# A hybrid trunk layer on one core: the first pass over the tokens in groups of four blocks

## The chip, the core and the metric

The kernel runs on one core of one Trainium2 chip. A core has five engines that run side by side, each with its own list of instructions in fixed order: TensorE (PE in the profile) multiplies matrices and transposes, VectorE (DVE), ScalarE (ACT) and GpSimd (POOL) work elementwise, and SyncE (SP) issues the transfers between memory and the core's on-chip memory (SBUF). PE writes its results to a small accumulation memory (PSUM) in banks of 128 x 512 floats; DVE and ACT read them from there. An engine that waits holds up everything behind it in its own list. The metric is the time of one execution on the device, in microseconds (us); lower is better.

## The reference, cut to what matters

One layer of a trunk over 2048 latent tokens and 256 context tokens of width 1024. Both are normalised, scaled and shifted, and one projection of the result `h` feeds two mixers, a gated delta net and a windowed attention; their outputs are gated, merged, projected and added to `x`.

```
h  = _rmsnorm(x, norm_w) * (1.0 + scale[:, None]) + shift[:, None]
hc = _rmsnorm(ctx, norm_w) * (1.0 + scale_c) + shift_c
...
qkv, beta_r, decay_r, kb, vb = _split_cols(h @ w_state, STATE_SIZES)
za, qb, zb, ga, gb = _split_cols(h @ w_rest, REST_SIZES)
...
kb = _axial_rope(_rmsnorm(kb.reshape(b, l, ATT_KV_HEADS, ATT_HD), k_norm_w), pos_row, pos_col)
```

The first pass, which the change touches, computes `h` for all tokens and from it the columns for beta, decay, and the attention's keys `kb` and values `vb`.

## The kernel before, in words

The tokens are 18 blocks of 128, two of the context and 16 of x. All products are made in split precision: each factor is a high part and a low part (the rounding's remainder), and three products (high x high, low x high, high x low) are summed in PSUM. `h` is kept on chip with the features on the partitions, as `hh` (high) and `hl` (low), one tile pair of [128, 8, 512] for each group of four blocks and one for the context.

At the start the modulation's `shift` and `scale` are computed from two halves of `w_mod` (16 loads of 512 KB, tile `wm`); the context's blocks are loaded and normalised meanwhile. Then the first pass runs, over pairs of blocks:

- `load_x` loads a block into an `xt` tile. There are four of these, shared by context and x.
- `norm_x` sums the block's squares, half a block on ACT (L295) and half on DVE (L298, both write only a throw-away tile `junk` and the sum `ss`), adds the two (POOL, L299), forms mean plus eps (POOL, L301) and the power -0.5 (POOL, L72, `rstd`), and scales the block in place (DVE, L303).
- `make_h` takes a pair: for each of the eight feature tiles PE transposes the two blocks into one PSUM bank (`hps`, four banks, L344), ACT evicts 128 x 256 with scale and shift into half of an `h32` tile (`h` in the profile, L345, two buffers), POOL rounds two feature tiles at once to `hh` (L347) and DVE takes the remainder `hl` (L348).
- `tm_dense` multiplies one block with 272 columns of `w_in`: 24 products (`tmps`, L374 to L376) into one of three accumulator banks.
- `state_pair` takes two blocks' accumulators: ACT copies beta and decay (`bg`, L431) and the values (`vst`, L433, remainder on DVE L434) and squares the keys (`sq`, L435); DVE sums, POOL forms the norm (`ssn`, L439 and L72), DVE multiplies (`xn`, L443, the last reader of the accumulators), DVE and POOL rotate (`t`, `cw`, L452 to L462), ACT and DVE split into `kh` (L464 to L466), PE transposes (`kt`, L472), ACT copies to `ks` (L473), and SP stores to `Vsp` and `Ksp`.

Behind the last block the weights of the next stage come in, and PE starts the long products for the convolutions, `lps` (L532 to L534).

The order of instructions on each engine is set when the program is built, by a scheduler that goes by its own estimates; tiles come from pools with fixed numbers of buffers, and a tile's next use waits for the last reader of its buffer.

## Time and profile before

| | |
|---|---|
| three runs | 2110.58, 2101.88, 2107.05 us; median 2107.05 |
| profiled execution, span from first to last instruction | 2106.8 us |
| mean granted PE clock | 0.981 |
| busy: PE, DVE, POOL, ACT | 1991.7, 1424.9, 773.2, 746.8 us |
| first pass: first and last product of a `tmps` kind | from 44.75 us to just ahead of 136.96 us |

The profiled execution has no time of its own beside its span; the span stands at the median of the runs. In the rows of the profile, a group is named by line, engine, operation and tile (`out<-in`), with its count; an arrow in a row of waits or at the end of a group names what the engine waited for last. Busy times of PE are modelled, since products overlap.

### The profile page before, as it was taken

To read this page: it belongs to the slowest core of one execution; us is meant where nothing else is said; L and a number is where in the kernel's file an instruction comes from. 1 tells how busy PE (TensorE), PEld (TensorE's weight loads), DVE (VectorE), ACT (ScalarE), POOL (GpSimd) and SP (SyncE) were. 2 spreads that over 40 slices of the span, in tenths; PEclk is the share of its full clock that TensorE was granted. 3 is DMA by queue.
4 is the path that set the end of the run, shared out by engine and by line. 5 is a ranking of instruction groups with operands and counts; after the bars stand their busy time and mean duration, and the time that the engine had idled before them with its cause. 6 is when DMAs were issued, how large, how long until landed. Compare 5 with 4: busy or idle time off the path is not lost.

```text
span 2106.8 us, 32857 instructions
## 1 busy us (share of the span) xinstructions
PE 1991.7 (95%) x11351; PEld 1647.6 (78%) x11351; DVE 1424.9 (68%) x2715; ACT 746.8 (35%) x1911; POOL 773.2 (37%) x919
## 2 busy tenths in 40 slices
PE   6999999999998799889979999999989999999999
PEld 3888888888986567667867888888868787878887
DVE  6888767767662799789846985634587777753322
ACT  6655555644440001001211223323575555441100
POOL 2852202355541355313322223322356343442321
PEclk8999999999999899999989999999999999999999
DMA  6552247755444533437667778763365545455542
GB/s 248 163 145 86 78 134 207 209 170 157 142 139 111 125 105 110 108 98 215 182 177 202 207 217 231 202 205 116 116 190 180 173 149 174 121 178 190 172 145 93
DMA packets 392591, 335.47 MB, mean 159 GB/s; under 512 B 83144, under 2 KB 318600, under 8 KB 392072
## 3 DMA queue, kind: packets, MB, share of 16 engines
q1 hardware_dynamic: 365000, 290.88, 48.1%
q10 hardware_dynamic: 27424, 42.48, 5.7%
q8 instruction: 90, 1.47, 0.3%
q14 instruction: 77, 0.63, 0.1%
HBM read 220.21 MB, written 111.49 MB: 157 GB/s over the span
## 4 chain that ended last, share of the span: by engine, by line
PE 66%; DMA 10%; DVE 9%; POOL 4%; SPq 4%; issue 4%; ACT 2%; POOLq 0%; DVEq 0%; ACTq 0%
PE rps L534 5%; PE rps L532 5%; PE rps L533 4%; PE lps L532 4%; PE lps L534 4%; PE lps L533 4%; PE ops L1272 3%; PE ops L1274 3%; PE ops L1273 3%; DMA wr<-in_w_in_dram 2%; PE pps L1187 2%; PE pps L1188 2%; PE pps L1189 2%; PE pt L922 2%; DVE N L735 2%
## 5 line engine op out<-in xcount | busy, mean ns | idle before, releaser
L532 PE MATMUL rps<-hh,wh 128*128 128x512 f32 x768 | 313.7, 409 | 6.2 <-DVE rt L798 4.9
L534 PE MATMUL rps<-hh,wl 128*128 128x512 f32 x768 | 311.3, 406 | 0.0
L533 PE MATMUL rps<-hl,wh 128*128 128x512 f32 x768 | 309.9, 403 | 0.0
L251 POOL TENSOR_SCALAR wh<-wr 128x512 fp32r<-128x512 f32 x120 | 103.7, 874 | 276.6 <-DMA wr<-in_w_in_dram 119.7
L796 ACT ACTIVATE rt<-rps 128x512 f32<-128x512 f32 x96 | 57.4, 598 | 386.9 <-PE rps L534 327.8
L532 PEld LDWEIGHTS rps<-hh,wh 128*128 128x128 f32 x768 | 147.3, 192 | 39.3 <-DVE rt L798 5.3
L534 PEld LDWEIGHTS rps<-hh,wl 128*128 128x128 f32 x768 | 147.2, 192 | 36.5 <-issue 2.0
L533 PEld LDWEIGHTS rps<-hl,wh 128*128 128x128 f32 x768 | 147.2, 192 | 32.7 <-issue 1.3
L532 PE MATMUL lps<-hh,wh 128*128 128x512 f32 (+1 forms) x448 | 171.9, 384 | 0.3 <-ACT y L632 0.3
L534 PE MATMUL lps<-hh,wl 128*128 128x512 f32 (+1 forms) x448 | 171.4, 383 | 0.0
L533 PE MATMUL lps<-hl,wh 128*128 128x512 f32 (+1 forms) x448 | 171.2, 382 | 0.0
L571 DVE SCALAR_TENSOR_TENSOR cacc<-y,cw,cacc 128x512 f32<-128x512 f32 (+1 forms) x224 | 161.5, 744 | 13.9 <-ACT cacc L569 10.8
L908 POOL TENSOR_SCALAR pr<-pr,sm 128x640 f32<-128x640 f32 (+1 forms) x128 | 99.2, 795 | 176.7 <-DVE sm L906 154.3
L252 DVE TENSOR_TENSOR wl<-wr,wh 128x512 fp32r<-128x512 f32 x120 | 96.6, 814 | 71.2 <-POOL wh L251 69.0
L926 DVE TENSOR_TENSOR pl<-pt,ph 128x512 fp32r<-128x512 f32 x156 | 106.7, 685 | 39.7 <-ACT ph L924 38.9
L924 ACT CAST ph<-pt 128x512 fp32r<-128x512 f32 x156 | 90.9, 585 | 113.0 <-PE pt L922 72.1
L898 DVE TENSOR_REDUCE sm<-sc 128x1 f32<-128x640 f32 (+1 forms) x128 | 101.7, 800 | 38.8 <-PE sc L896 38.2
L735 DVE TENSOR_TENSOR N<-N,btmp 128x62 f32<-128x62 f32 (+30 forms) x124 | 120.9, 975 | 2.8
L733 DVE TENSOR_TENSOR btmp<-N 128x62 f32<-128x62 f32 (+30 forms) x124 | 119.4, 963 | 3.0
L900 ACT ACTIVATE pr<-sc,sm 128x640 f32<-128x640 f32 (+1 forms) x128 | 100.2, 784 | 49.0 <-DVE sm L899 39.4
L1187 PE MATMUL pps<-yh,wph 128*128 128x512 f32 x256 | 104.0, 410 | 7.3 <-ACT yh L1169 5.3
L1188 PE MATMUL pps<-yl,wph 128*128 128x512 f32 x256 | 102.9, 402 | 0.2 <-DVE yl L1170 0.2
(312 smaller groups left out, 5061.0 us busy)
## 6 DMA issues: line engine op xcount, KB each, us to landing
wr<-in_w_in_dram SPq DMA_DIRECT2D x120, 256.0 KB
kw<-Ksp SPq DMA_DIRECT2D x28, 384.0 KB
x<-vsp SPq DMA_DIRECT2D x36, 256.0 KB
k<-ksp SPq DMA_DIRECT2D x34, 256.0 KB
kT<-kTsp SPq DMA_DIRECT2D x34, 256.0 KB
wm<-in_w_mod_dram SPq DMA_DIRECT2D x16, 512.0 KB
xt<-in_x_dram SPq DMA_DIRECT2D x16, 512.0 KB
dtl<-Dsp SPq DMA_DIRECT2D x32, 256.0 KB
```

Of the source, the lines that this page charges most:

```text
L251: G.tensor_scalar(wh[:, k:k + 4], wr, 1.0, 1.0, op0=ALU.mult, op1=ALU.mult)
L532: T.matmul(ps, lhsT=wh[:, k], rhs=xh[:, k], start=k == 0, stop=False)
L533: T.matmul(ps, lhsT=wh[:, k], rhs=xl[:, k], start=False, stop=False)
L534: T.matmul(ps, lhsT=wl[:, k], rhs=xh[:, k], start=False, stop=k == kt - 1)
L571: V.scalar_tensor_tensor(a, y[:, t:t + n], cw[:, m, t:t + 1], a, op0=ALU.mult, op1=ALU.add)
L733: V.tensor_tensor(tv, A[:, m + 1:, m].unsqueeze(2).to_broadcast([h1 + n, r, m]), A[:, m, 0:m].unsqueeze(1).to_broadcast([h1 + n, r, m]), o ...
L735: V.tensor_tensor(A[:, m + 1:, 0:m], A[:, m + 1:, 0:m], tv, op=ALU.add)
L898: V.tensor_reduce(sm[:, h, 0:1], s_, axis=AX.X, op=ALU.max)
L900: S.activation(p[:, h, :W + 256], s_, AF.Exp, scale=0.125, bias=sm[:, h, 1:2], accum_out=sm[:, h, 2:3])
L926: V.tensor_tensor(pl, pt, f32(ph), op=ALU.subtract)
L1187: T.matmul(ps, lhsT=wh[:, k, ms], rhs=hs[k], start=k == 0, stop=False)
L1188: T.matmul(ps, lhsT=wh[:, k, ms], rhs=ls[k], start=False, stop=False)
```

## The change

The first pass goes over groups of four blocks, four times, and not over pairs, eight times. `load_x` can be given the place to load to. `norm_x` takes all blocks of a group: ACT alone sums the squares of each block in one 128 x 1024 operation, the two small POOL operations and the power run once for the group, and then DVE scales the four blocks. `make_h` transposes four blocks into a bank, evicts 128 x 512 at once, and takes one feature tile in an `h32` tile (for the context still two, of 256). Group 0 and group 3 are loaded into the four `xt` tiles; groups 1 and 2 are loaded into the memory that later holds `hh` and `hl` of group 3, which is free until then. `tm_dense` and `state_pair` are as they were, two pairs to a group.

```diff
-        def load_x(c):
-            xt = px.tile([128, D], F32, name="xt")
+        def load_x(c, xt=None):
+            if xt is None:
+                xt = px.tile([128, D], F32, name="xt")
...
-        def norm_x(c, xt):
-            ss = px.tile([128, 2], F32, name="ss")
-            for j in range(2):
-                junk = px.tile([128, 512], BF16, name="junk", bufs=1)
-                xs = xt[:, j * 512:(j + 1) * 512]
-                if j == 0:
-                    S.activation(junk, xs, AF.Square, accum_out=ss[:, j:j + 1])
-                else:
-                    junk2 = px.tile([128, 512], BF16, name="junk2", bufs=1)
-                    V.scalar_tensor_tensor(junk2, xs, 1.0, xs, op0=ALU.mult, op1=ALU.mult, accum_out=ss[:, j:j + 1])
-            G.tensor_tensor(ss[:, 0:1], ss[:, 0:1], ss[:, 1:2], op=ALU.add)
-            ss = ss[:, 0:1]
-            G.tensor_scalar(ss, ss, 1.0 / D, EPS, op0=ALU.mult, op1=ALU.add)
-            rsq(rstd[:, c:c + 1], ss)
-            V.tensor_scalar(xt, xt, rstd[:, c:c + 1], None, op0=ALU.mult)
+        def norm_x(c, xts):
+
+            n = len(xts)
+            ss = px.tile([128, 4], F32, name="ss", bufs=2)
+            for j, xt in enumerate(xts):
+                junk = px.tile([128, D], BF16, name="junk", bufs=1)
+                S.activation(junk, xt, AF.Square, accum_out=ss[:, j:j + 1])
+            G.tensor_scalar(ss[:, :n], ss[:, :n], 1.0 / D, EPS, op0=ALU.mult, op1=ALU.add)
+            rsq(rstd[:, c:c + n], ss[:, :n])
+            for j, xt in enumerate(xts):
+                V.tensor_scalar(xt, xt, rstd[:, c + j:c + j + 1], None, op0=ALU.mult)
...
-            for k in range(0, KT, 2):
-                h32 = px.tile([128, 2, 256], F32, name="h32", bufs=2)
-                for i in range(2):
+            per = 512 // n
+            for k in range(0, KT, per):
+                h32 = px.tile([128, per, n], F32, name="h32", bufs=2)
+                for i in range(per):
...
-                    S.activation(h32[:, i, :n], ps[:, :n], AF.Identity, scale=modA[:, k + i, cc:cc + 1],
+                    S.activation(h32[:, i], ps[:, :n], AF.Identity, scale=modA[:, k + i, cc:cc + 1],
                                  bias=modB[:, k + i, cc:cc + 1])
-                G.tensor_scalar(hi[:, k:k + 2], h32[:, :, :n], 1.0, 1.0, op0=ALU.mult, op1=ALU.mult)
-                V.tensor_tensor(lo[:, k:k + 2], h32[:, :, :n], f32(hi[:, k:k + 2]), op=ALU.subtract)
+                G.tensor_scalar(hi[:, k:k + per], h32, 1.0, 1.0, op0=ALU.mult, op1=ALU.mult)
+                V.tensor_tensor(lo[:, k:k + per], h32, f32(hi[:, k:k + per]), op=ALU.subtract)
...
-        for gi in range(8):
-            xts = []
-            for j in range(2):
-                c = NCB + gi * 2 + j
-                with tc.issue_after(wm_dma.ins):
-                    xts.append(load_x(c))
-                norm_x(c, xts[j])
-            o = gi % 2 * 256
-            make_h(xts, hh[gi // 2][:, :, o:o + 256], hl[gi // 2][:, :, o:o + 256], 0)
-            if gi == 7:
+        for gi in range(4):
+            c = NCB + gi * 4
+            homes = [None] * 4
+            if gi in (1, 2):
+                four = hB2.tile([128, 4, D], F32, name="xt4", tag="hh3" if gi == 1 else "hl3")
+                homes = [four[:, j] for j in range(4)]
+            if gi == 3:
+                hh[3] = hB2.tile([128, KT, 512], F32R, name="hh3", tag="hh3")
+                hl[3] = hB2.tile([128, KT, 512], F32R, name="hl3", tag="hl3")
+            with tc.issue_after(wm_dma.ins):
+                xts = [load_x(c + j, homes[j]) for j in range(4)]
+            norm_x(c, xts)
+            make_h(xts, hh[gi], hl[gi], 0)
+            if gi == 3:
...
-            c = NCB + gi * 2
-            state_pair(c, [tm_dense(c + j, wh, wl, NST) for j in range(2)])
+            for i in (0, 2):
+                state_pair(c + i, [tm_dense(c + i + j, wh, wl, NST) for j in range(2)])
```

The scheduler's order changes with it, up to the last product of the pass; behind that, every engine's list is what it was, apart from line numbers. Three places follow.

ACT, around the context's finished products (`bg`, `vst`, `sq` of the context's two blocks read its finished products). Before:

```order
L345 ACTIVATE h_650<-hps,modB,modA 128x256
L295 ACTIVATE junk,ss<-xt 128x512
L345 ACTIVATE h_661<-hps,modB,modA 128x256 x2
L345 ACTIVATE h_672<-hps,modB,modA 128x256
L431 COPY bg<-tmps 128x16
L433 CAST vst<-tmps 128x2x64
```

Now (`xt` is group 0, `xt_902` group 1, `xt_1188` group 2; `h_636` and `h_645` are group 0's first evictions):

```order
L431 CAST vst<-tmps 128x2x64
L433 ACTIVATE sq<-tmps 128x128
L296 ACTIVATE junk,ss<-xt 128x1024 x2
L296 ACTIVATE junk,ss<-xt_902 128x1024
L462 CAST kh<-xn 128x4x128
L296 ACTIVATE junk,ss<-xt_902 128x1024 x3
L296 ACTIVATE junk,ss<-xt_1188 128x1024
L343 ACTIVATE h_636<-hps,modB,modA 128x512
L343 ACTIVATE h_645<-hps,modB,modA 128x512
```

Squares and evictions of pair 0 stood ahead of the context's copies; now seven squares, two of them group 0's, stand behind these and ahead of group 0's first eviction.

DVE, from the scaling of the first blocks of x on. Before (`hl_447` is the context's, `hl_179` that of the first four blocks):

```order
L348 TENSOR_TENSOR hl_447<-h_487,hh_446 128x512
L298 SCALAR_TENSOR_TENSOR junk_809,ss<-xt 128x512
L303 TENSOR_SCALAR xt<-xt,rstd 128x1024
L348 TENSOR_TENSOR hl_179<-h_650,hh_178 128x2x256
L303 TENSOR_SCALAR xt<-xt,rstd 128x1024
L434 TENSOR_TENSOR vst<-tmps,vst 128x2x64
L348 TENSOR_TENSOR hl_179<-h_661,hh_178 128x2x256
```

Now:

```order
L300 TENSOR_SCALAR xt<-xt,rstd 128x1024 x4
L463 TENSOR_TENSOR kh<-xn,kh 128x4x64
L464 CAST kh<-kh 128x4x64
L300 TENSOR_SCALAR xt_902<-xt_902,rstd 128x1024 x4
L346 TENSOR_TENSOR hl_179<-h_636,hh_178 128x512
L346 TENSOR_TENSOR hl_179<-h_645,hh_178 128x512
L346 TENSOR_TENSOR hl_179<-h_654,hh_178 128x512
L300 TENSOR_SCALAR xt_1188<-xt_1188,rstd 128x1024 x4
L346 TENSOR_TENSOR hl_179<-h_663,hh_178 128x512
```

The four scalings of group 1 stand ahead of group 0's first remainder, and those of group 2 ahead of its fourth.

PE, ahead of the fourth block's products of group 0 (the two products shown first are the last of its other three blocks). Now:

```order
L373 MATMUL tmps<-wh,hl_179 128x272
L374 MATMUL tmps<-wl,hh_178 128x272
L342 MATMUL hps<-ident,xt_902 128x128 x16
L342 MATMUL hps<-ident,xt_1188 128x128 x4
L372 MATMUL tmps<-wh,hh_178 128x272
```

The last transposes of group 1 and the first of group 2, which need banks that the evictions of group 1 free, stand ahead of the fourth block's products.

More of the change, by code (lines that the diff above doesn't have):

```diff
@@ L320, in _hybrid @@
                 if j == 0 and 2 <= k < 2 + NCB:
-                    c = k - 2
-                    pre.append(load_x(c))
-                    norm_x(c, pre[c])
+                    pre.append(load_x(k - 2))
+                    if len(pre) == NCB:
+                        norm_x(0, pre)
             mrow = pm.tile([4, D], F32, name="mrow", tag="wm", bufs=7)
@@ L344, in make_h @@
                         T.transpose(ps[:, j * 128:(j + 1) * 128], xt[:, (k + i) * 128:(k + i + 1) * 128], ident)
-                    S.activation(h32[:, i, :n], ps[:, :n], AF.Identity, scale=modA[:, k + i, cc:cc + 1],
+                    S.activation(h32[:, i], ps[:, :n], AF.Identity, scale=modA[:, k + i, cc:cc + 1],
                                  bias=modB[:, k + i, cc:cc + 1])
-                G.tensor_scalar(hi[:, k:k + 2], h32[:, :, :n], 1.0, 1.0, op0=ALU.mult, op1=ALU.mult)
-                V.tensor_tensor(lo[:, k:k + 2], h32[:, :, :n], f32(hi[:, k:k + 2]), op=ALU.subtract)
+                G.tensor_scalar(hi[:, k:k + per], h32, 1.0, 1.0, op0=ALU.mult, op1=ALU.mult)
+                V.tensor_tensor(lo[:, k:k + per], h32, f32(hi[:, k:k + per]), op=ALU.subtract)
         pm_.__exit__(None, None, None)
-        hpool("hB2", [3])
+        hB2 = hpool("hB2", [])
         hpool("hC", [4])
```

## Prediction

> **What bounds the kernel now.** I read the page first, then the windows over the first 175 us, then the waits of the first pass. In the page's span and chain of waits the reader sees that TensorE (PE) carries two thirds of the chain that ended last.
>
> ```profile
> span 2106.8 us, 32857 instructions
> ...
> PE 66%; DMA 10%; DVE 9%; POOL 4%; SPq 4%; issue 4%; ACT 2%; POOLq 0%; DVEq 0%; ACTq 0%
> ```
>
> The windows (length, then busy time and count of each engine, granted clock, DMA) show where PE has slack. From 150 us on it is busy all the time; in the first pass over the tokens DVE and POOL are nearly as busy as PE.
>
> ```profile
> 75.00:100.00 25.00, 23.29 (x172) 20.53 (x170) 22.37 (x51) 17.22 (x50) 21.79 (x34) 1.00 0.55 165
> ...
> 150.00:175.00 25.00, 25.00 (x130) 20.78 (x128) 24.08 (x53) 11.57 (x27) 7.28 (x6) 1.00 0.30 91
> ...
> 54.50:136.90 82.40, 74.21 (x560) 67.22 (x559) 69.77 (x161) 55.50 (x155) 67.45 (x99) 1.00 0.51 162
> ```
>
> The changed program's instruction lists differ from the old ones only up to the end of this pass; behind the last product of the pass every engine has the same instructions in the same order. As PE is full from there on, whatever the pass's end moves, the end of the kernel moves too. So the question is when PE starts its first `lps` product, which was at 136.96:
>
> ```profile
> 136.96 0.28 PE L532 MATMUL lps<-hh,wh 128*128 128x256 f32 x1
> ```
>
> Waits from 41 to 141 us (total us, times, longest): PE loses little to each single cause.
>
> ```profile
> ACT h L345 <- DVE hl L348: 10.8, 13, 1.7
> ...
> PE tmps L374 <- POOL hh L347: 2.0, 3, 1.4
> ...
> PE tmps L374 <- DVE xn L443: 1.7, 3, 1.1
> ```
>
> **What the parts cost on their engines.** Groups of the first 260 us, and last, for a slope, one of the whole run (busy us, mean ns, idle before); then three pieces of ScalarE's (ACT's) timeline (start, length):
>
> ```profile
> L345 ACT ACTIVATE h<-hps,modB,modA 128x256 f32<-128x256 f32 x72 | 36.7, 564 | 13.5 <-DVE hl L348 10.8 <-PE hps L344 2.4 <-PE tmps L376 0.3
> L348 DVE TENSOR_TENSOR hl<-h,hh 128x512 fp32r<-128x512 f32 x36 | 28.9, 815 | 5.6 <-POOL hh L347 5.5
> L347 POOL TENSOR_SCALAR hh<-h 128x512 fp32r<-128x512 f32 x36 | 26.2, 732 | 6.9 <-ACT h L345 6.6
> L303 DVE TENSOR_SCALAR xt<-xt,rstd 128x1024 f32<-128x1024 f32 x18 | 17.6, 976 | 5.0 <-POOL rstd L72 5.0
> L314 ACT CAST wmh<-wm 128x1024 fp32r<-128x1024 f32 x16 | 16.6, 1047 | 9.2 <-DMA wm<-in_w_mod_dram 3.5 <-DVE wml L315 2.2 <-PE hps L344 1.7
> L298 DVE SCALAR_TENSOR_TENSOR junk<-xt 128x512 bf16<-128x512 f32 x18 | 13.1, 728 | 2.3 <-DMA xt<-in_x_dram 2.2
> L72 POOL TENSOR_TENSOR rstd<-ss,expo 128x1 f32<-128x1 f32 x18 | 11.8, 655 | 1.3
> L72 POOL TENSOR_TENSOR ssn<-ssn,expo 128x4 f32<-128x4 f32 x9 | 10.4, 1157 | 0.7
> L632 ACT COPY y<-lps 128x512 f32<-128x512 f32 x16 | 9.3, 581 | 13.2 <-PE lps L534 11.5 <-DVE cacc L573 1.7
> L299 POOL TENSOR_TENSOR ss<-ss 128x1 f32<-128x1 f32 x18 | 7.5, 419 | 17.7 <-DVE junk L298 14.5 <-ACT junk L295 1.7 <-DVE hl L348 1.2
> L301 POOL TENSOR_SCALAR ss<-ss 128x1 f32<-128x1 f32 x18 | 7.0, 388 | 1.6
> L439 POOL TENSOR_SCALAR ssn<-ssn 128x4 f32<-128x4 f32 x9 | 5.0, 553 | 3.3 <-DVE ssn L438 2.8
> L632 ACT COPY y<-lps 128x256 f32<-128x256 f32 x4 | 1.5, 363 | 1.8 <-PE lps L534 1.5 <-DVE cacc L573 0.3
> ```
>
> ```profile
> L924 ACT CAST ph<-pt 128x512 fp32r<-128x512 f32 x156 | 90.9, 585 | 113.0 <-PE pt L922 72.1 <-PE av L928 40.0
> ```
>
> ```profile
> 42.88 1.93 ACT L345 ACTIVATE h<-hps,modB,modA 128x256 f32<-128x256 f32 x4
> ...
> 50.03 0.62 ACT L295 ACTIVATE junk<-xt 128x512 bf16<-128x512 f32 x1
> ...
> 50.65 0.55 ACT L345 ACTIVATE h<-hps,modB,modA 128x256 f32<-128x256 f32 x1
> ```
>
> *Evictions.* Four of 256 in a row take 1.93 us, 0.48 each; another 256 columns cost 581 - 363 = 0.22. I take 0.70 for 128x512, between 0.58 (the copy of that size) and 0.96 (two old ones). 64 become 32: ACT saves 64 x 0.48 - 32 x 0.70 = 8.3 us.
>
> *Squares.* DVE's half goes: 13.1 us and its accumulator reads. On ACT a square took 0.62 from its start to the next instruction (50.03 to 50.65); 512 more columns cost 1047 - 585 = 0.46, so 1.08 (bounds 1.05, the 1024 cast, and 1.24, two old steps), 18 times 0.46 more: 8.3 us, which eats what the evictions gave.
>
> *The small chain.* Three operations a block (0.42 + 0.39 + 0.66 us on POOL) become two a group, of a form that exists as `ssn`: 0.55 + 1.16 = 1.71 us. POOL saves 18 x 1.46 - 5 x 1.71 = 17.8 us.
>
> *PE* keeps its transposes and products; loads keep their bytes. So the sums favour the change, but they are off PE, and what counts is in which order the rest now reaches PE.
>
> **The path to the first group.** Before, pair 0 was squared, scaled and partly transposed while the context's products ran. The changed lists put the squares of blocks 2 and 3 on ACT behind the context's `bg`, `vst` and `sq`, which wait for the context's last product, and nothing of the group can be transposed before all four are scaled. The rows for the start, SP's load, ACT's first copy behind the context's products, and the second copy of pair 1 for comparison:
>
> ```profile
> 45.79 0.80 SPq L286 DMA_DIRECT2D xt<-in_x_dram  x2
> ...
> 49.53 0.69 DVE L298 SCALAR_TENSOR_TENSOR junk<-xt 128x512 bf16<-128x512 f32 x1 [0.83 <-DMA xt<-in_x_dram]
> ...
> 54.54 0.16 ACT L431 COPY bg<-tmps 128x16 f32<-128x16 f32 x1
> ...
> 75.48 0.18 ACT L431 COPY bg<-tmps 128x16 f32<-128x16 f32 x1
> ```
>
> A load takes 3.7 us to its reader (45.79 to 49.53). Step by step, times in us of the span:
>
> - 53.3: the context's products end, 54.5 less the ten transposes that stood between them (0.09 each and the change of kind).
> - 55.1: `bg`, `vst`, `sq` (1.8, estimated). 57.3: two squares. 59.0: POOL's chain.
> - ACT goes on with one square of group 1, `kh` (0.6), three more squares of group 1 (to 62.2) and one of group 2: 63.3, and only then group 0's first eviction. PE has had next to nothing for nine us.
> - DVE's list holds group 1's four scalings ahead of group 0's first `hl`: 62.2 + 1.7 (POOL) = 63.9, four of 0.98: 67.8, first `hl` 68.5. With two `h32` buffers the third eviction waits for it.
> - The same again for group 2: last square 70.3, POOL 72.0, scalings 75.9, fourth `hl` 76.6. Group 3's loads wait for group 0's last transposes (72.3): landed 76.0; ACT's four squares and five evictions, 4.3 + 3.5, are through at 83.8, the last square at 83.1; POOL 84.8; scalings 88.7; group 1's second `hl` 89.4.
> - Behind that stand the sum over `sq` (89.8), POOL (91.5) and `xn`, which frees an accumulator: group 0's fourth block starts at 91.8. With three accumulators it can't earlier, and PE's list puts twenty transposes of groups 1 and 2 ahead of it besides.
>
> PE may be cold by then. When it restarted before, at the context's products, its granted clock was 0.50 and came back within the second of these windows (the clock is the third number from the end):
>
> ```profile
> 44.75 0.80 PE L374 MATMUL tmps<-wh,hh 128*128 128x272 f32 x2
> ...
> 44.00:46.00 2.00, 1.98 (x9) 1.41 (x8) 2.00 (x2) 1.64 (x4) 1.33 (x2) 0.50 0.39 130
> ...
> 48.00:50.00 2.00, 2.00 (x14) 2.00 (x14) 1.16 (x2) 1.32 (x3) 0.62 (x1) 0.70 0.98 377
> ```
>
> A mean of 0.70 is half rate until 49.2, so a restart at 44.75 ran 4.4 us at half rate and lost 2.2 us, which I add (between nothing and 2.2). (The Trainium skill, "TensorE: Matmul & The Clock Gate", Part 1, lets the half rate end after a busy window of about 3.4 us. By that rule it would be 1.7, the sum 0.5 lower; the row here has 4.4 for 3.4, and I go by the row.)
>
> The scalings weigh three times four in this path. Over x's 16 blocks (min, median, max ns):
>
> ```profile
> L303 DVE TENSOR_SCALAR xt<-xt,rstd x16: 740/1104/1224, 40.6 to 119.6; 128x1024 f32<-128x1024 f32 x16
> ```
>
> I take the mean, 0.98; the bounds are 0.74 and 1.10, 2.9 us less or 1.4 more over the path. (The Trainium skill, "GPSIMD Engine Reference", Specifications, has POOL and DVE share their SBUF interfaces, with contention when DVE runs in a two-port mode. POOL mostly waits while a group is scaled, so by that rule it is 0.74 and the sum is 2.9 us lower; the spread of the row agrees, but here no row separates the cases.)
>
> **The rest of the pass.** Spacing of products and of transposes on PE, and the time from a block's last product to the `xn` that frees its accumulator:
>
> ```profile
> 54.51 0.60 PE L344 MATMUL hps<-ident,xt 128*128 128x128 f32 x4
> 54.86 0.37 PE L374 MATMUL tmps<-wh,hh 128*128 128x272 f32 x1
> ...
> 62.05 0.29 PE L375 MATMUL tmps<-wh,hl 128*128 128x272 f32 x1
> ...
> 64.06 0.29 PE L376 MATMUL tmps<-wl,hh 128*128 128x272 f32 x1
> ```
>
> ```profile
> 86.58 0.16 ACT L431 COPY bg<-tmps 128x16 f32<-128x16 f32 x1
> ...
> 92.28 0.49 DVE L443 TENSOR_TENSOR xn<-tmps,ssn 128x128 f32<-128x128 f32 x2
> ```
>
> Sixteen products in 2.01 us are 0.126 each; four transposes in 0.35 are 0.09. The fourth block ends at 91.8 + 3.0 + 2.2 = 97.0, where the old kernel was at 75.5: 21.5 us late. Twelve blocks are left: 288 products 36.3, 60 transposes of x and 52 of keys 10.1, some 25 changes of kind at 0.08 2.0: 48.4, where the old kernel took 136.96 - 75.48 = 61.5, since squares, small chains and scalings of all later groups are done by then and DVE and POOL no longer fill the period. I add 2 us for the block that waits for the second pair's `xn` (5.7 us behind its product in the rows, 3.5 at best). 97.0 + 50.4 = 147.4, 10.4 behind the old 136.96. The profiled run stands at the median (2106.8 and 2107.05), so the forecast is 2106.8 + 10.4, some **2117 us**.
>
> Its own range: all low bounds (scalings 2.9; eight evictions of the path at 0.12 less and thirteen squares at 0.03 less, 1.4; no cold clock 2.2; no wait 2) take 8.5 us off, 2109; the high ones (scalings 1.4, squares 13 x 0.16 = 2.1, evictions 8 x 0.26 = 2.1, twice the wait 2) put 7.6 on, 2125.
>
> **Rivals.** *The relief wins.* If group 0's first eviction comes by 60 us (group 1's squares in fact not in its way), PE is left with 48.4 us of products for 16 blocks, 11.5 of transposes of x, 5.8 of keys and 3 of changes, 69 us, against 82.4 in the window; less a start gap of some 7, a gain of 6.4: 2100. For it: DVE and POOL are the fullest beside PE there. Against: the lists put seven squares ahead of that eviction. *The old pace stays.* If each pair still waits for `xn` behind other work, the twelve blocks take 61.5 again, and the end is 97.0 + 61.5 = 158.5: 21.5 us later, 2128. It decides if the 5.7 us of the rows stay; against it is that what stood in that way on DVE and POOL is gone. *Nothing changes:* late start and faster rest cancel if the fourth block starts by 81; 2107. The change surely does what it says, as the lists show.
>
> **Chances.** Forecast 0.62, relief 0.10, no change 0.13, old pace 0.15. A measurement of this kernel tells about 0.5%, 10.5 us, from no change: 2096.5 to 2117.6. The forecast stands close to that edge; somewhat under half of it lies beyond. Slower 0.15 + 0.28 = 0.43; faster only in the best part of the relief, 0.04; same 0.53. The range that leaves out the best of the relief and the worst of the old pace: 2104 to 2128.
>
> **What would show it.** Right: PE nearly idle from about 53 to 62 us, ACT squaring meanwhile; group 0's first `hl` behind group 1's scalings near 68; the first `lps` product near 147; from 150 us on the same times shifted. The fourth block's products near 92 test the middle step, twelve blocks in 50 us the last. Wrong: the first `lps` product before 137, or a difference that arises after the pass.

## The result, and the profile after

The changed kernel takes 2121.06 us (median of 7 runs, 2119.74 to 2133.27); the kernel before, beside it, 2110.46 (7 runs, 2101.88 to 2115.72). The ratio is 1.0068, with a 95% interval of 1.0049 to 1.0088: slower, by some 14 us by this ratio and by 10.6 us by the two medians. The interval leaves out no change; its lower end lies at the half per cent that the prediction took as the least that a measurement of this kernel can tell from no change. The forecast was 2117 and a shift of 10.4 us. The profiled run took 2126.94 us, 6 us above the median, so the stages below are compared by their starts and not by the span.

The page of the changed kernel, span and shares of the chain that ended last: PE still carries nearly two thirds.

```profile
span 2124.9 us, 32729 instructions
...
PE 65%; DVE 10%; DMA 8%; SPq 4%; POOL 4%; issue 4%; ACT 1%; POOLq 0%; DVEq 0%; ACTq 0%
```

Where the time came in is seen from the first `lps` product, which was at 136.96, and from the first `rps` product behind it (start, length). After:

```profile
152.60 0.28 PE L534 MATMUL lps<-hh,wh 128*128 128x256 f32 x1
...
628.87 0.40 PE L534 MATMUL rps<-hh,wh 128*128 128x512 f32 x1
```

and before:

```profile
614.40 0.40 PE L532 MATMUL rps<-hh,wh 128*128 128x512 f32 x1
```

The first pass ends 15.6 us late, and 476 us later the kernel is still 14.5 late. The loss arises in the pass and is carried along almost unchanged. Behind that the two profiles drift: the last weight load of the form `rps<-hh,wh` is 21.3 us late (1553.1 against 1531.8) and the end of the span 18.1. But the stretch from the first of these loads to the last took anything from 915.6 to 931.9 us in the profiles of the kernels below, whose code is the same there, so one pair of profiles doesn't show a later loss. The windows of the changed kernel (length, busy time and count of PE, its weight loads, DVE, ACT, POOL, granted clock, DMA):

```profile
75.00:100.00 25.00, 17.94 (x129) 16.41 (x126) 18.28 (x33) 14.94 (x32) 13.56 (x18) 0.93 0.28 101
...
150.00:175.00 25.00, 24.84 (x141) 21.11 (x140) 18.56 (x65) 9.28 (x23) 3.43 (x5) 1.00 0.49 100
97.00:152.50 55.50, 48.88 (x397) 47.38 (x396) 38.69 (x95) 28.20 (x72) 33.02 (x46) 1.00 0.39 117
...
55.00:152.60 97.60, 75.78 (x568) 72.32 (x569) 66.39 (x142) 57.71 (x130) 52.61 (x73) 0.91 0.37 122
```

In the pass PE has 75.8 us of work in 97.6, where it had 74.2 in 82.4. Its idle time went from 8.2 to 21.8 us: 13.6 of the 15.6. DVE (66.4) and POOL (52.6) are now far from full, and PE is idle all the same. What it waits for from 55 to 152.6 us (total us, times, longest) makes up nearly all of the 21.8; the 6.8 us are the gap ahead of the context's key transposes and group 0's first transposes:

```profile
PE kt L470 <- ACT kh L462: 6.8, 1, 6.8
PE tmps L372 <- DVE xn L441: 6.1, 6, 1.5
PE hps L342 <- ACT h L343: 5.2, 3, 3.9
PE tmps L373 <- DVE hl L346: 3.6, 3, 2.6
```

The groups of operations in the first 260 us show that the savings on the other engines came in about as their sums said, or larger (POOL's small chain of the norms went from 26.3 to 6.1 us, a saving of 20.2 where 17.8 were forecast; DVE's scalings fell by 3.1, which was not forecast):

```profile
L343 ACT ACTIVATE h<-hps,modB,modA 128x512 f32<-128x512 f32 x32 | 24.4, 782 | 10.0 <-DVE hl L346 10.0
...
L296 ACT ACTIVATE junk<-xt 128x1024 bf16<-128x1024 f32 x18 | 19.0, 1056 | 8.8 <-DMA xt<-in_x_dram 8.2 <-DMA xt<-in_ctx_dram 0.4
...
L300 DVE TENSOR_SCALAR xt<-xt,rstd 128x1024 f32<-128x1024 f32 x18 | 14.5, 863 | 6.7 <-POOL rstd L72 6.6
...
L72 POOL TENSOR_TENSOR rstd<-ss,expo 128x4 f32<-128x4 f32 x4 | 4.1, 1014 | 0.3
```

### The profile page after: what moved, and what is told of

It reads as the page before. It is cut to its first block, busy times and chain, and to the rows that moved or that the text cites. A ratio compares the mean times of both kernels' runs of the same rounds, so it can differ in the third digit from the quotient of the medians.

```text
span 2124.9 us, 32729 instructions
## 1 busy us (share of the span) xinstructions
PE 1994.9 (94%) x11351; PEld 1652.2 (78%) x11351; DVE 1411.8 (66%) x2679; ACT 747.6 (35%) x1879; POOL 754.6 (36%) x875
## 4 chain that ended last, share of the span: by engine, by line
PE 65%; DVE 10%; DMA 8%; SPq 4%; POOL 4%; issue 4%; ACT 1%; POOLq 0%; DVEq 0%; ACTq 0%
PE rps L536 4%; PE lps L536 4%; PE lps L534 4%; PE lps L535 4%; PE rps L534 4%; PE rps L535 4%; PE ops L1274 3%; PE ops L1276 3%; PE ops L1275 3%; DVE N L737 3%; DVE btmp L735 2%; PE pt L924 2%; DMA wr<-in_w_in_dram 2%; PE pps L1189 2%; PE pps L1190 2%
## 5 line engine op out<-in xcount | busy, mean ns | idle before, releaser
L252 DVE TENSOR_TENSOR wl<-wr,wh 128x512 fp32r<-128x512 f32 x120 | 95.7, 808 | 76.4 <-POOL wh L251 75.5
```

## The experiments

All kernels below are compared with the kernel before, run beside them. The second column is ACT's first copy (`bg`) of the fourth block of group 0, the third that of the last block of the pass; `lps` and `rps` are the starts of the first such products in the one profiled run of each. ACT's copy can come up to 2.4 us behind PE's last product of the block (99.5 against 97.1 in the change, 82.6 against 80.2 in e13). "Group 0 done" also leaves different amounts of work behind it: of the 96 transposes of the last twelve blocks, 60 are left in the change, 82 before, 96 in e10. Where the order of instructions at the pass's end changes, a few key transposes of the last pair may stand ahead of `lps` or behind it; `rps` is the fairer mark there, to some 2 us (the way from `lps` to `rps` takes 475.8 to 480.0).

| kernel | group 0 done | last block | `lps` | `rps` | ratio to before (95%) |
|---|---|---|---|---|---|
| before | 75.5 | 137.7 | 136.96 | 614.40 | 1 |
| the change | 99.5 | 153.4 | 152.60 | 628.87 | 1.0068 (1.0049 to 1.0088) |
| e1_after_h | 87.9 | 154.8 | 154.30 | 630.74 | 1.0089 (1.0059 to 1.0120) |
| e3_pair_chain_sq | 75.7 | 138.3 | 138.38 | 615.95 | 1.0009 (0.9992 to 1.0026) |
| e5_half_sq | 97.4 | 151.7 | 150.93 | 627.59 | 1.0098 (1.0068 to 1.0128) |
| e6_acc4 | 87.0 | 145.0 | 151.48 | 628.61 | 1.0088 (1.0054 to 1.0122) |
| e7_ac4 | 87.0 | 144.9 | 145.00 | 623.47 | 1.0051 (1.0026 to 1.0075) |
| e9_before_ac4 | 75.0 | 137.2 | 137.71 | 614.33 | 1.0007 (0.9997 to 1.0016) |
| e4_pairs0 | 82.1 | 149.0 | 148.82 | 626.01 | 1.0060 (1.0032 to 1.0088) |
| e8_pairs_ac4 | 74.3 | 140.0 | 143.16 | 621.89 | 1.0038 (1.0022 to 1.0054) |
| e10_order_ac4 | 79.0 | 147.1 | 151.59 | 631.60 | 1.0080 (1.0054 to 1.0106) |
| e11_all | 76.9 | 145.2 | 150.19 | 628.92 | 1.0060 (1.0036 to 1.0084) |
| e13_pairs_early | 82.6 | 143.2 | 142.12 | 618.89 | 1.0054 (1.0035 to 1.0073) |
| e14_pairs_early_ord | 76.2 | 142.7 | 142.75 | 618.52 | 1.0025 (1.0010 to 1.0041) |

### Is it the queueing of later groups? (e1_after_h)

```diff
-            norm_x(c, xts)
-            make_h(xts, hh[gi], hl[gi], 0)
+            with tc.issue_after(hend[0].ins) if hend else nullcontext(), \
+                    tc.issue_after(hend[1].ins) if hend else nullcontext():
+                norm_x(c, xts)
+            hend = make_h(xts, hh[gi], hl[gi], 0)
```

`make_h` returns its last eviction and its last `hl`. Expected:

> The changed kernel, but the squares and scalings of each later group stand behind the last eviction and the last `hl` of the group before; everything else as changed (wide evictions, one chain a group, late loads). Theory 1 (later groups' norms queued ahead of group 0 cost the start): the scalings of group 0 end near 64 as before, its first eviction comes near 64.5, its first `hl` near 66.5 instead of 69.9, its eight evictions run through by 70, and its fourth block ends near 81 instead of 96.6. Each later group then needs 4.7 (squares) + 1.9 (POOL) + 2.7 (scalings) + 1.5 + 5.5 (evictions) = 16.3 us, about PE's own 16.5 us a group, so the first lps product is near 81 + 51 = 132 to 137 and the time near the old kernel's, 2100 to 2112. Rival A (a group of four is late because all four blocks are needed before the first transpose, and the wide forms cost): the fourth block stays beyond 90, the first lps product beyond 146, the time at 2118 or more. Rival B (the three accumulators and the wait for `xn` set a pace of 55.9 us for the last twelve blocks wherever they start): 81 + 56 = 137 or later, with waits of PE for `xn` of 6 us or more.

The timeline of this kernel (start, length, engine): first and last `hl` of group 0, the first scaling of group 1, and ACT's copies behind the fourth block of each group.

```profile
65.67 0.69 DVE L346 TENSOR_TENSOR hl<-h,hh 128x512 fp32r<-128x512 f32 x1 [3.62 <-POOL hh L345]
...
74.09 0.69 DVE L346 TENSOR_TENSOR hl<-h,hh 128x512 fp32r<-128x512 f32 x1 [0.51 <-POOL hh L345]
...
79.66 0.76 DVE L300 TENSOR_SCALAR xt<-xt,rstd 128x1024 f32<-128x1024 f32 x1 [0.63 <-POOL rstd L72]
...
87.89 0.17 ACT L430 COPY bg<-tmps 128x16 f32<-128x16 f32 x1
...
108.96 0.16 ACT L430 COPY bg<-tmps 128x16 f32<-128x16 f32 x1
...
132.98 0.17 ACT L430 COPY bg<-tmps 128x16 f32<-128x16 f32 x1
...
154.85 0.16 ACT L430 COPY bg<-tmps 128x16 f32<-128x16 f32 x1
```

The start moved the way theory 1 said: the eight `hl` of group 0 run from 65.7 to 74.8, where the changed kernel has them from 69.9 to 83.7, and the fourth block is 11.6 us earlier (9.5 by PE's last product), though at 87.9 and not near 81. But nothing of it reaches the end. Each later group now takes 21 to 24 us. Squares and scalings that are no longer done under the work of the group before explain only a part: PE waits 4.1 us for group 1's scalings, and from 87.7 to 154.3 its waits are 8.2 us in all, 1.0 of them for scalings, against 6.6 in the change's last twelve blocks. For the rest it is busy, 58.3 us against 49.0. It has 80 transposes of x left there where the change has 60, and its granted clock was 0.57 from 126 to 130 us and from 150 to 154. Theory 1 explains the late start and not the lost time; rival A's late fourth block did not come, though its late end did (154.3, and 2128.4 us), and of rival B's waits for `xn` only 2.2 us. What the queueing costs at the head, this kernel pays behind.

### Are the squares on ACT or the small chain to blame? (e3_pair_chain_sq, e5_half_sq)

In e3 the kernel before, with its pairs and loads, takes over the whole-row squares and one chain of small operations for each pair:

```diff
-                norm_x(c, xts[j])
+            norm_x(NCB + gi * 2, xts)
...
+            for j, xt in enumerate(xts):
+                junk = px.tile([128, D], BF16, name="junk", bufs=1)
+                S.activation(junk, xt, AF.Square, accum_out=ss[:, j:j + 1])
```

> The kernel before with its pairs of blocks, 128x256 evictions and load order, and two parts of the change alone: whole-row squares all on ACT, and one chain of small operations for each pair (context too). Theory 1 (only the queueing of groups of four lost the time): DVE loses 13.1 us of squares and POOL half of its small chain without any later group standing ahead, so the first lps product comes at 137 or a few us earlier (131 to 137), and the time is that of before or up to 6 us under it. Rival C (the squares on ACT cost the time, 8.3 us more on an engine that PE waits for): the first lps product at 142 to 150, the time 5 to 13 us over that of before.

In e5 the changed kernel halves its squares again:

```diff
-                S.activation(junk, xt, AF.Square, accum_out=ss[:, j:j + 1])
+                    if j == 0:
+                        S.activation(junk, xs, AF.Square, accum_out=ss[:, j, i:i + 1])
+                    else:
+                        junk2 = px.tile([128, 512], BF16, name="junk2", bufs=1)
+                        V.scalar_tensor_tensor(junk2, xs, 1.0, xs, op0=ALU.mult, op1=ALU.mult, accum_out=ss[:, j, i:i + 1])
```

> The changed kernel with one part undone: each square is halved between ACT and DVE again, three small operations a group. Rival C (squares on ACT): group 0's first eviction waits for half the squaring, about 4 us earlier, and the first lps product moves from 152.6 to 146 or less, the time to 2114 or less. Theory 1 (queueing): DVE's list then holds eight half squares of 0.73 us as well as the four scalings ahead of group 0's second `hl`, so what ACT gains DVE loses; the first lps product stays within 149 to 158 and the time within 2117 to 2127.

Rival C falls in both: e3 is the kernel before within its interval, e5 is no better than the change (its `lps` is 1.7 us earlier, within what theory 1 gave; its time, 2129.6, is above what either theory gave, with the change's ratio at the edge of its interval, and nothing in its pass shows why). The window of e3's pass is the more telling result:

```profile
55.00:138.40 83.40, 74.87 (x558) 67.50 (x557) 61.78 (x138) 59.80 (x155) 55.44 (x74) 0.98 0.48 155
```

DVE went from 69.8 to 61.8 us and POOL from 67.5 to 55.4, and PE's idle time is still 8.5. Theory 1's hope of a gain, an end before 137, was wrong as well: the busy time of those two engines is not what PE waits for in the pass of pairs.

### Do three accumulators set the pace? (e6_acc4, e7_ac4, e9_before_ac4)

e6 takes a bank from the transposes for a fourth accumulator, and gives it back behind the pass:

```diff
-    psum_phase("left", acc=3)
-    psum_phase("right", hps=4, kt=1)
+    psum_phase("left", acc=4)
+    psum_phase("right", hps=3, kt=1)
```

> The changed kernel with four accumulators and three transpose buffers in the first pass instead of three and four (the accumulators are set back to three behind the pass). Rival B (PE's last twelve blocks wait for `xn` to free one of three accumulators): the 6 us of PE's waits for `xn` between 97 and 150 go, and the first lps product comes near 146 to 148, the time near 2115. Theory 1 (DVE and POOL were late from the queueing at the start, and the wait for the accumulator only shows it): the wait moves to the next thing that they make, `hl` or `kh`, and the first lps product stays within 2 us of 152.6, the time near 2121.

The pass's last block came 8.4 us earlier, but the order of instructions then put the last pair's key transposes ahead of the first `lps`, PE waited for their copies, and `lps` is where it was. So e7 keeps the accumulators and uses the bank as one of its own for each fourth block:

```diff
-    psum_phase("right", hps=4, kt=1)
+    psum_phase("right", hps=3, kt=1, ac4=1)
...
-            ps = acc([128, 512], name="tmps")
+            ps = psum("ac4" if c % 4 == 1 and "ac4" in pst["right"][2] else "acc", [128, 512], name="tmps")
```

> The changed kernel with three transpose buffers instead of four and the bank as an accumulator of its own for every fourth block, so that the fourth block of a group need not wait for `xn` of its first pair (nothing is reopened behind the pass, as it was with four accumulators). Theory 2 (PE's waits for `xn`, 6.1 us from 97 to 152, are the term of the last twelve blocks that was set too low): the last product of the pass ends at 145 to 147 and the first lps product follows at once, 6 us or more ahead of 152.6; the time 2111 to 2116. Rival E (the wait goes to the next thing that DVE and POOL make): the first lps product within 3 us of 152.6, the time 2118 to 2122.

The waits of PE in the changed kernel from 97 to 152 us (total us, times, longest):

```profile
PE tmps L372 <- DVE xn L441: 6.1, 6, 1.5
PE tmps L373 <- DVE hl L346: 0.5, 1, 0.5
```

and in e7 from 87 to 145:

```profile
PE hps L342 <- ACT h L343: 2.5, 2, 1.5
PE tmps L373 <- DVE hl L346: 1.9, 4, 1.1
PE tmps L372 <- ACT vst L431: 0.6, 1, 0.6
```

The waits for `xn` are gone, the first `lps` product is 7.6 us earlier, the first `rps` product 5.4. From 55 us to `lps` PE is idle for 12.8 us instead of 21.8. Not all of this falls in the last twelve blocks: group 0's fourth block, which stands behind an `xn` too, ends 11.7 us earlier by PE's products, with 90 transposes left to do instead of 60. Theory 2 holds for the accumulators as a whole, rival E falls; the time (2118.86, expected 2111 to 2116) shows less of it, and its interval doesn't tell it from the change by itself. The same edit on the kernel before:

> The kernel before with three transpose buffers and an accumulator of its own for every fourth block, nothing else. Theory 2 holds for groups of four alone: PE there waited 1.7 us for `xn` in 82, so the first lps product is within 2 us of 137 and the time that of before. Rival F (three accumulators set the pace of the pass in both kernels, and the pairs hid it under small waits for `hh` and `hl`): the pass ends 5 us or more earlier, the first lps product at 132 or less, the time 5 us under that of before.

```profile
PE tmps L375 <- DVE hl L348: 6.6, 13, 0.8
PE tmps L374 <- POOL hh L347: 1.9, 6, 0.7
```

These are its waits from 55 to 137 us: none is for `xn` any more, but those for `hl` grew from 1.9 to 6.6, and the end is the same. Rival F falls: this exchange of a bank, which takes one from the transposes, gains time with groups of four and none in the kernel before. That three accumulators cost nothing with any pairs is not shown (see e14 below).

### Can the start be mended without a price? (e4_pairs0, e8_pairs_ac4, e10_order_ac4, e11_all)

e4 lets group 0 alone go as two pairs:

```diff
-            norm_x(c, xts)
-            make_h(xts, hh[gi], hl[gi], 0)
+            if gi == 0:
+                for i in (0, 2):
+                    norm_x(c + i, xts[i:i + 2])
+                    make_h(xts[i:i + 2], hh[0][:, :, i * 128:i * 128 + 256], hl[0][:, :, i * 128:i * 128 + 256], 0)
+            else:
...
```

> The changed kernel, but the first group alone goes as two pairs (squares, chain, 128x256 evictions and transposes of a pair at a time, squares still whole rows on ACT); groups 1 to 3 stay as changed, with their early loads. Theory 1 (the time is lost where the first group waits for four blocks and for later groups' squares and scalings): group 0's fourth block ends near 77 as in the kernel before, instead of 97 to 99; the last twelve blocks keep the changed kernel's 54 to 56 us; the first lps product comes near 131 to 134, the time 3 to 6 us under that of before. Rival D (the start only hides a shortage: what is not squared and scaled ahead of group 0 has to be done during the twelve blocks, which then go at 61 us or slower as in the kernel before and with serial norms): group 0 near 77, but the first lps product at 138 or later, the time not under that of before.

Group 0 was done 17 us earlier than in the change, `lps` came 3.8 us earlier: rival D, by its times. e8 adds the accumulator of e7, and the order of e1 for group 1 alone:

> Both repairs together on the changed kernel: the first group as two pairs, the squares and scalings of group 1 behind the last eviction and last `hl` of group 0, and an accumulator of its own for every fourth block. Theories 1 and 2 together: group 0's fourth block ends near 76, twelve blocks in 48.4 to 51, the first lps product at 125 to 130, the time 7 to 12 us under that of before. Rival D (what is not prepared ahead has to be done in the twelve blocks): group 1 waits for its norm, 10 us or more between group 0's last product and group 1's first, the first lps product at 136 or later, no gain over before.

It is the best of the kernels with groups of four, and still 6 to 8 us behind before: rival D again, with 10 us between group 0's last product (73.6) and group 1's first (83.9). Its timeline on DVE between the scalings of group 1 and its first `hl`s shows what is in the way now:

```profile
77.56 2.74 DVE L300 TENSOR_SCALAR xt<-xt,rstd 128x1024 f32<-128x1024 f32 x4 [0.63 <-POOL rstd L72]
...
83.45 0.69 DVE L346 TENSOR_TENSOR hl<-h,hh 128x512 fp32r<-128x512 f32 x1 [0.78 <-POOL hh L345]
84.43 3.92 DVE L300 TENSOR_SCALAR xt<-xt,rstd 128x1024 f32<-128x1024 f32 x4 [0.29 <-POOL rstd L72]
...
88.61 1.28 DVE L346 TENSOR_TENSOR hl<-h,hh 128x512 fp32r<-128x512 f32 x2
...
90.81 3.45 DVE L300 TENSOR_SCALAR xt<-xt,rstd 128x1024 f32<-128x1024 f32 x4 [0.71 <-POOL rstd L72]
94.18 1.28 DVE L346 TENSOR_TENSOR hl<-h,hh 128x512 fp32r<-128x512 f32 x2
```

Groups 2 and 3 are scaled between the first `hl`s of group 1: five of these take from 83.4 to 95.5. Mended for group 0, the queueing hits group 1. e10 takes it away everywhere (the edits of e1 and e7 together):

> The changed kernel with both of the single edits that were run before: the squares and scalings of each later group behind the last eviction and last `hl` of the group before, and an accumulator of its own for every fourth block. Alone the first gave a first lps product at 154.3 (group 0 ended at 87.9 instead of 99.5, and then each group waited for its norm and for `xn`), the second 145.0. Theory 3 (two causes that cover each other: queued norms delay group 0 by 12 us, and the wait for `xn` of three accumulators costs 6 to 9 us wherever it falls): group 0 ends at 77 to 80, later groups take 17 to 18 us each, the first lps product comes at 130 to 135, the time 2 to 7 us under that of before. Rival D (norms that don't run ahead have to run between the groups): group 0 at 77 to 80, but 20 us or more for each later group, first lps product at 139 or later, no gain over e7's 145 beyond 6 us and none over before.

ACT's copies behind the fourth block of each group, and the windows of the pass and of its groups 2 and 3:

```profile
78.97 0.17 ACT L430 COPY bg<-tmps 128x16 f32<-128x16 f32 x1 [1.03 <-PE tmps L375]
...
100.13 0.23 ACT L430 COPY bg<-tmps 128x16 f32<-128x16 f32 x1
...
124.21 0.23 ACT L430 COPY bg<-tmps 128x16 f32<-128x16 f32 x1
...
147.06 0.17 ACT L430 COPY bg<-tmps 128x16 f32<-128x16 f32 x1 [0.51 <-PE tmps L375]
```

```profile
55.00:151.60 96.60, 79.98 (x569) 72.75 (x569) 66.20 (x141) 59.11 (x128) 56.45 (x72) 0.91 0.33 106
...
100.10:124.20 24.10, 21.47 (x146) 19.82 (x146) 16.48 (x36) 15.64 (x36) 14.03 (x19) 0.86 0.24 78
124.20:147.00 22.80, 19.47 (x147) 17.30 (x146) 18.49 (x40) 11.69 (x28) 14.81 (x19) 1.00 0.39 116
```

Group 0 is done 20 us earlier than in the change, and 14 of these are lost again at 21.2, 24.1 and 22.9 us a group (19.1, 18.3 and 16.6 in the change). Another 4.3 go behind the last block, where PE waits for `xn` ahead of `lps`. Theory 3 falls, and rival D's times came. Its reason, norms that have to run between the groups, is not what PE's waits show: from 79.0 to 147.1 they are 7.0 us in all, 2.2 of them for scalings, against 6.6 in the change's last twelve blocks. Instead PE is busy for 60.3 us against 49.0. All 96 transposes of x are still to do there (17.6 us, against 7.6 for the 60 of the change), and group 2 ran at a granted clock of 0.86: 2.0 us more than group 3 for about as many products and transposes (146 and 147). Over the whole pass PE is idle for 16.6 us, 5.2 less than in the change, and busy for 80.0, 4.2 more. How the extra busy time divides between the clock and work that comes in small pieces was not tested. e11 adds the pair start and halved squares to e10:

> The same order and accumulators, the first group as two pairs, and each square halved between ACT and DVE, to shorten the norm of a group by some 2 us where it stands on PE's path. Theory 3: group 0 ends at 74 to 77, later groups at 16.5 to 17.5 each, the first lps product at 125 to 130, the time 7 to 12 us under that of before. Rival D: later groups at 20 us or more each, 137 or later, time that of before or above.

Group 0 at 76.9, the last block at 145.2, then 4.7 us of waiting for `xn`, and `rps` where the change has it: rival D's times again, with 21 to 24 us a group.

### The size of the group, or the early loads? (e13_pairs_early, e14_pairs_early_ord)

e13 keeps the change's loads and has pairs everywhere, with the halved squares of e5:

```diff
-            norm_x(c, xts)
-            make_h(xts, hh[gi], hl[gi], 0)
+            for i in (0, 2):
+                norm_x(c + i, xts[i:i + 2])
+                make_h(xts[i:i + 2], hh[gi][:, :, i * 128:i * 128 + 256], hl[gi][:, :, i * 128:i * 128 + 256], 0)
```

> The changed kernel with its early loads in fours into the last group's memory and its order of loads, but pairs of blocks throughout: 128x256 evictions, transposes, squares (halved between ACT and DVE) and one chain of small operations for each pair; three accumulators. It tells the early loads, by which later blocks are ready to be squared ahead of their turn, from the size of the group. Theory 4 (early loads let later blocks' squares and scalings queue ahead, whatever the group's size): group 0 ends at 80 to 84 as with a pair start, the first lps product at 144 to 150, 7 us or more over before. Theory 5 (the size of the group: the first transposes, evictions and products wait for four blocks): group 0 near 76, the first lps product within 3 us of 137, the time that of before.

Group 0 is where theory 4 put it, the end between the two theories. With e4 it gives a ladder of first `rps` products: before 614.4; pairs with early loads and one chain a pair 618.9 (+4.5); groups 1 to 3 as fours, with whole squares 626.0 (+7.1); group 0 as a four too, the change, 628.9 (+2.9). The larger part of the loss comes with the size of the group (of the 7.1, some 1.5 may be the squares, by e5). The times of these kernels (1.0054, 1.0060, 1.0068) lie in the same order, but their intervals overlap; the ladder rests on one profile for each rung. By `lps` the steps are 5.2, 6.7 and 3.8.

e14 binds the squares and scalings of a pair in e13 to the last eviction and last `hl` of the pair two before:

> Pairs throughout with the early loads in fours and one chain of small operations for each pair, as in the run of pairs before (first lps product at 142.1, group 0 at 82.6), but the squares and scalings of a pair stand behind the last eviction and last `hl` of the pair two before it, which is as far ahead as the memory allowed in the kernel before. Theory 4 (early loads cost only because squares and scalings of later blocks, ready early, are queued ahead): group 0's fourth block ends at 75 to 77, the first lps product at 133 to 138, the time that of before to 4 us under it. Rival G (the loads themselves, in fours and early, or one chain for a pair cost the 5 us, not the order): group 0 at 80 or later, the first lps product at 140 to 144, the time 4 us or more over that of before.

PE's longest wait from 76 to 143 us:

```profile
PE tmps L380 <- DVE xn L449: 4.7, 5, 1.4
```

Group 0 comes at 76.2, as theory 4 said, and `lps` at 142.75, as rival G said. Again an earlier start (6.4 us by ACT's copy, 4.1 by PE's products) is paid back. Why pairs with early loads stay 4 us behind the old pairs, when they may run no further ahead, is not settled. The waits for `xn` are the largest difference seen: 4.7 us here, 0.2 before from 76 to 137. Pairs with early loads and an accumulator of its own for every fourth block would test that, and were not run. No kernel here beats the one before.

## Where the prediction was right, and where it failed

**What bounds, and where the difference arises.** Right: PE's start of `lps` moves the end, and the shift is nearly the same at 152 and at 629 us (15.6 and 14.5). The forecast time is nearer than the sum behind it. The two medians lie 10.6 us apart, where 10.4 were forecast, but the pass, from which the 10.4 were worked out, ended 15.6 late; and of the 4 us between 2117 and 2121, 3.7 come from the kernel before, which the forecast took at 2106.8 and which had a median of 2110.5 beside the change.

**The path to the fourth block.** The timeline of the changed kernel, with its steps in the prediction's order:

```profile
54.98 0.17 ACT L429 COPY bg<-tmps 128x16 f32<-128x16 f32 x1 [0.41 <-PE tmps L374]
...
58.86 1.06 ACT L296 ACTIVATE junk<-xt 128x1024 bf16<-128x1024 f32 x1 [0.18 <-DMA xt<-in_x_dram]
...
60.04 1.06 ACT L296 ACTIVATE junk<-xt 128x1024 bf16<-128x1024 f32 x1
...
61.41 2.74 DVE L300 TENSOR_SCALAR xt<-xt,rstd 128x1024 f32<-128x1024 f32 x4 [2.47 <-POOL rstd L72]
...
66.24 1.43 ACT L343 ACTIVATE h<-hps,modB,modA 128x512 f32<-128x512 f32 x2
66.52 3.45 DVE L300 TENSOR_SCALAR xt<-xt,rstd 128x1024 f32<-128x1024 f32 x4 [1.70 <-POOL rstd L72]
...
69.89 1.28 DVE L346 TENSOR_TENSOR hl<-h,hh 128x512 fp32r<-128x512 f32 x2
...
78.08 1.06 ACT L296 ACTIVATE junk<-xt 128x1024 bf16<-128x1024 f32 x1 [4.22 <-DMA xt<-in_x_dram]
...
86.60 3.44 DVE L300 TENSOR_SCALAR xt<-xt,rstd 128x1024 f32<-128x1024 f32 x4
...
92.77 0.49 DVE L441 TENSOR_TENSOR xn<-tmps,ssn 128x128 f32<-128x128 f32 x2 [0.99 <-POOL ssn L72]
...
93.26 0.57 PE L372 MATMUL tmps<-wh,hh 128*128 128x272 f32 x1
```

Right in each step of the order: seven squares ahead of group 0's first eviction (63.3 forecast, 66.2 found), group 1's scalings ahead of its first `hl` (68.5 as an end, 69.9 as a start), group 3's square behind its load (76.0 and 78.1), its scalings ahead of `xn`, and the fourth block behind `xn` (91.8 and 93.3). Until 93.26 PE was busy with the last of the twenty transposes that its list puts ahead of this block, so the rows don't tell which of the two held it; e7, without the wait for `xn`, has the block 11.7 us earlier. Its products end at 97, where the sum had 97.0. That is in part luck: the context's products ended 1.3 us late (ACT's copy behind them starts at 55.0) and the load landed 2 us late, while the scalings took 0.69 to 0.86 each and not 0.98, and the cold clock cost less than 2.2.

**Sizes.** Two wide evictions take 1.43 us (0.72 each, 0.70 forecast); squares follow each other at 1.18 (1.08 forecast, 1.24 the upper bound); POOL's chain of a group is 0.2 to 0.4 + 1.0 us (1.71 forecast).

**The step that failed** is the last term of the sum: "I add 2 us for the block that waits for the second pair's `xn`". It was mis-sized. PE's own work in the twelve blocks was right (48.9 us in the window against 48.4), but six waits for `xn` cost 6.1 us and one for `hl` 0.5, so that the twelve blocks took 55.6 us instead of 50.4. I had counted one block of the pass as waiting; with three accumulators every block stands behind the `xn` of the block three before it, and one in two had to wait. e7 takes these waits out, and `lps` comes 7.6 us earlier; as a part of that comes from group 0's fourth block, it bounds the term rather than measures it. With 6.6 in place of 2 the sum would have been 2106.8 + 15.0 = 2122.

**The rivals.** The relief did not win; by e3, what it relieves is not what PE waited for. The old pace did not stay either (55.6 against 61.5 us), but the experiments show that pace and start are not two separate terms, as the prediction had them (a late start of +21.5, a faster rest of -11). What is done ahead of group 0's fourth block is not left for the twelve blocks behind it: squares, scalings and transposes. e1, e4, e10 and e11 bring group 0 in 12 to 23 us earlier than the change and start `lps` from 1.7 us later to 3.8 us earlier; e14 does the same to e13 with 4 to 6 us and keeps none. Moved work is not the whole account. From 55 us to `lps` PE is idle for 21.8 us in the change and for 17.5, 16.6 and 15.5 in e1, e10 and e11, but for 563 to 569 products and transposes it is busy for 81.8, 80.0 and 79.7 instead of 75.8. So what these kernels gain in idle time, PE loses in busy time, a part of it at half its clock behind gaps. A kernel that closes these gaps was not run.

**Scalings and clock.** While group 0 is scaled, POOL does nothing from 61.4 to 65.2, and a scaling takes 0.69 us; the four of group 1, with POOL's `hh` beside them from 67.1 to 68.8, take 0.86 on average. The prediction used 0.98 and named 0.74 as the case without contention. (The Trainium skill, "GPSIMD Engine Reference", Specifications, has POOL and DVE share their SBUF interfaces; these rows agree.) On the clock, the windows around the fourth block (granted clock third from the end):

```profile
91.50:93.20 1.70, 1.69 (x8) 1.42 (x9) 0.71 (x5) 0.78 (x1) 1.62 (x3) 0.50 0.00 0
93.20:94.40 1.20, 1.20 (x7) 1.20 (x7) 1.20 (x6) 0.00 (x0) 0.78 (x3) 0.50 0.00 0
94.40:96.00 1.60, 1.60 (x14) 1.60 (x14) 1.60 (x3) 0.78 (x1) 1.24 (x2) 0.98 0.00 0
```

Half rate held for 2.9 us of work, and over half of it fell on transposes that came before `xn` was there; the products lost 0.6 us, not 2.2. The prediction's 4.4 us were misread: its own window from 44 to 46 us shows PE busy for 1.98 of 2.00, and the half rate held from 43.4, when PE restarted with transposes, to 49.2, so for 5.8 us. At the changed kernel's first restart it held longer still, from 61.8 to 70.4 us at 0.50, with PE busy for 7.4 of these 8.6. (The Trainium skill, "TensorE: Matmul & The Clock Gate", Part 1, has a busy window of about 3.4 us; only the 2.9 is near it.)

## What to carry to other kernels

Where engines read their queues in order and one of them (here PE) is nearly full, work taken off the others is worth nothing until it shortens the chain that the full engine waits for; look for its waits, not for the busiest helper. A larger group lengthens that chain at every boundary: count how many blocks can be in flight (accumulators) before the first one's last reader is through, and charge the wait to every group, not once. And where later groups are prepared early, don't book the late start and the faster rest as two separate terms. Here an earlier first group left more work for the later ones, and an order that opened gaps between the groups gave PE a lower clock behind them.

## What the runs showed of the hardware

DVE's scaling of a 128x1024 tile takes 0.69 us with POOL idle and 0.86 on average where POOL's `hh` runs beside some of them in the same kernel, and 0.98 (busy mean) in the kernel before, where POOL was fuller. PE's granted clock is 1.00 from 55 to 137 us in the kernel before, where it never waits longer than 1.4 us; in the change it fell to 0.50 in the gaps ahead of 61.8 and 91.5 us, which were 6.8 and 3.9 us long, and full clock came back 8.6 and 2.9 us behind the restart. The wide eviction and the wide square cost about what the nearest rows gave, the wider small operations less (1.2 us for 1.71).
